# MLP weight sums on VectorE from blocks at hand, and second-product operands split early and kept in DRAM

## The chip, the cores and the metric

The kernel runs on one core of one Trainium2 chip. The metric is the device time of one execution in microseconds (us); smaller is better. The engines are PE (TensorE), DVE (VectorE), ACT (ScalarE), POOL (GpSimd) and SP, which only issues DMAs.

## What is computed

One encoder layer on 512 tokens of width 2048 (16 heads of 128, MLP width 8192), all in float32:

```python
a = rms_norm(x, norm_mix)
h = x + stick_breaking_mixer(a, w_qkv, w_o)
h = h + jnp.square(jax.nn.relu(rms_norm(h, norm_mlp) @ w1)) @ w2
out = rms_norm(h, final_norm)
```

The change touches only the MLP, the third line: a first product of 512x2048 by 2048x8192, a squared ReLU, and a second product of 512x8192 by 8192x2048.

## The kernel before

Every float32 operand of a matmul is split into a high part and a remainder, both rounded to the matmul's type: ACT casts the high part (`whi`, `11h`), DVE subtracts it for the low part (`wlo`, `11l`). A product is then three matmuls, high by high, high by low and low by high (`mm3`, L146 to L150). Attention and its output projection take the first 790 us or so. The MLP follows in two stages.

**Seven products for eight.** Both stages use a Strassen-like scheme: operands are cut in 2x2 blocks, and a unit of work makes seven products of sums of blocks instead of eight of blocks. `ORDER` (L378) lists the seven: the name of the left operand (`11`, `12`, `s1`, `s4`, `s2`, `s3`, `22`), the chain of weights, the PSUM accumulator, and what is added to the weights afterwards. A unit's positions are called p0 to p6 here. Stage 1 (`unit_1`) is 16 units, each 512 of the 8192 columns, 48 matmuls of 256 columns in a product. Stage 2 (`unit_2`) is 8 steps c of two units each (q = 0, 1), 24 matmuls of 512 columns in a product. Units run in order, u0 to u15 and then 16 more; PE runs the products one after the other (`run2`, L437).

**Weights.** A unit loads three of its four weight blocks by SP (`Unit.fetch`): chain a starts with block (0,0) in tile `ra`, b with (1,1) in `rb`, c with (1,0) in `raw`, each as two tiles of 128x1024 (512 KB). `split2` (L409) keeps two products ahead of PE. It casts and subtracts each tile into the pool `wp` of six buffers (a product uses four), and when an entry of `ORDER` says so it adds the next block into the raw tile by an accumulating DMA from POOL's queue:

```python
if more:
    nc.gpsimd.dma_start(raw, u.block(*more, pc), accum_op=ALU.add)
```

So `ra` is p0's weights, and after one, two and three additions those of p2, p4 and p6; `rb` is p3's, and after one addition p5's; `raw` is p1's. A unit has 8 such DMAs. The next unit's tiles are fetched after the splits of p0 (a), p1 (c) and p5 (b).

**Left operands.** In stage 1 they are made once, in 56 of the 72 tiles of the pool `tp`, and stay until u15. A unit's four result blocks go through ReLU and square in `evac_1` (L467) and are stored by ACT's queue to `a_dram` (`store`, L476), 4 tiles of 256 KB. In stage 2 the blocks of step c+1 come back during step c (`mix_a`, L361: tiles `ain`, loaded by SP), and `mix_tasks` (L325) makes the seven operands of each of two halves: four DVE sums (`mix`, L338), seven ACT casts (L332) and seven DVE subtractions (L333). These tasks stand in the list `side`, from which `run2` takes one after each half product. For c = 0 they run during u15, as do the loads of the residual h (`load_h`).

**End.** `load_gain` loads the last norm's gains in the next to last unit, and POOL scales them (L556); `final` (L528) uses POOL too (L535).

The order of each engine's instructions is set at build time by a scheduler which puts them where it expects their inputs to be ready; on the chip each engine and each queue takes its own in order. SP's loads wait there for the buffer they write.

Of the kernel before, what the change touches and what calls it, by code (L numbers as in the profile page):

```python
# [8 lines left out]
F32 = mybir.dt.float32  # L9
F32R = mybir.dt.float32r  # L10
AF = mybir.ActivationFunctionType
ALU = mybir.AluOpType
# [3 lines left out]
P = 128  # L16
S = 512
D = 2048
DF = 8192
# [21 lines left out]
def trunk_kernel(  # L41
# [13 lines left out]
    nc = tc.nc  # L55
# [4 lines left out]
    acc_a = ctx.enter_context(tc.tile_pool(name="acc_a", bufs=4, space=PSUM))  # L60
    dram = ctx.enter_context(tc.tile_pool(name="dram", bufs=1, space=DRAM))
    h_dram = {(tb, n): dram.tile([P, W], F32, name=f"h_{tb}_{n}") for tb in range(NT) for n in range(4)}
    a_dram = {(u, th, kh): dram.tile([P, 2, 256], F32, name=f"a_{u}_{th}_{kh}")
              for u in range(DF // 512) for th in range(2) for kh in range(2)}

    def slot(dt=F32, name="t"):
        return tp.tile([P, W], dt, name=name, tag="t")

    def f(ap):
        return ap.bitcast(F32)  # L70
# [152 lines left out]
    half_in = {}  # L223
    mixed = {}
# [96 lines left out]
    def two(name):  # L321
        return (slot(F32R, name + "h").rearrange("p (i q) -> p i q", q=256),
                slot(F32R, name + "l").rearrange("p (i q) -> p i q", q=256))

    def mix_tasks(key, blocks):  # L325


        got = {}

        def keep(name, a):  # L330
            hi, lo = two(name)
            nc.scalar.copy(hi, a)  # L332
            nc.vector.tensor_tensor(out=lo, in0=a, in1=f(hi), op=ALU.subtract)  # L333
            mixed.setdefault(name, {})[key] = (hi, lo)

        def mix(name, a, b, op):
            t = slot(F32, "mix").rearrange("p (i q) -> p i q", q=256)
            nc.vector.tensor_tensor(out=t, in0=a, in1=b, op=op)  # L338
            got[name] = t

        def s1():
            mix("s1", blocks(1, 0), blocks(1, 1), ALU.subtract)
            keep("s1", got["s1"])

        def s4():
            mix("s2", got["s1"], blocks(0, 0), ALU.subtract)
            mix("s4", blocks(0, 1), got["s2"], ALU.add)
            keep("s4", got["s4"])

        def s3():  # L350
            mix("s3", blocks(0, 0), blocks(1, 0), ALU.subtract)
            keep("s3", got["s3"])

        return [lambda: keep("11", blocks(0, 0)), lambda: keep("12", blocks(0, 1)), s1, s4,
                lambda: keep("s2", got["s2"]), s3, lambda: keep("22", blocks(1, 1))]

    def mix_h(jp):

        return mix_tasks(jp, lambda th, kh: half_in[th, jp + 4 * kh])

    def mix_a(c, pl):  # L361

        got = {}

        def fetch():
            for th, kh in ((0, 0), (0, 1), (1, 0), (1, 1)):
                got[th, kh] = slot(F32, "ain").rearrange("p (i q) -> p i q", q=256)
                nc.sync.dma_start(got[th, kh], a_dram[2 * c + pl, th, kh])

        return fetch, mix_tasks((c, pl), lambda th, kh: got[th, kh])  # L370

# [4 lines left out]
    ORDER = (  # L378
        ("11", "a", "x", (0, 1)),
        ("12", "c", "z", None),  # L380
        ("s1", "a", "y", (1, 1)),
        ("s4", "b", "y", (0, 1)),
        ("s2", "a", "x", (1, 0)),
        ("s3", "b", "x", None),
        ("22", "a", "x", None),
    )
# [20 lines left out]
    done = {"split": 0}  # L407

    def split2(upto):  # L409

        while done["split"] < min(upto, 7 * len(units2)):
            i = done["split"]
            u, (_, chain, _, more) = units2[i // 7], ORDER[i % 7]
            parts = []
            for pc in range(2):
                raw = u.raw[chain, pc]
                hi = wp.tile([P, u.jn, u.width], F32R, name="whi", tag="w")
                lo = wp.tile([P, u.jn, u.width], F32R, name="wlo", tag="w")
                nc.scalar.copy(hi, raw)  # L419
                nc.vector.tensor_tensor(out=lo, in0=raw, in1=f(hi), op=ALU.subtract)  # L420
                parts.append((hi, lo))
                if more:
                    nc.gpsimd.dma_start(raw, u.block(*more, pc), accum_op=ALU.add)  # L423
            ready[i] = parts
            done["split"] += 1
            nxt = units2[i // 7 + 1] if i // 7 + 1 < len(units2) else None
            if nxt:
                if i % 7 == 0:
                    nxt.fetch("a")
                elif i % 7 == 1:  # L430
                    nxt.fetch("c")
                elif i % 7 == 5:
                    nxt.fetch("b")

    side = []
# [30 lines left out]

    def evac_1(u):  # L467

        got = {}

        def tile_of(name):
            if name not in got:
                got[name] = slot(F32, name).rearrange("p (i q) -> p i q", q=256)
            return got[name]

        def store(t, th, kh):  # L476
            nc.scalar.activation(t, t, AF.Square)
            nc.scalar.dma_start(a_dram[u, th, kh], t)

        def go(p, s, ps):  # L480
            if p == 0:
                nc.scalar.copy(tile_of("p1")[:, s, :], ps)
            elif p == 1:
                c = tile_of("p1")
                nc.vector.tensor_tensor(out=c[:, s, :], in0=ps, in1=c[:, s, :], op=ALU.add)
                if s:
                    nc.scalar.activation(c, c, AF.Relu)
                    store(c, 0, 0)
            elif p == 2:
                nc.scalar.copy(tile_of("y1")[:, s, :], ps)  # L490
            elif p == 3:
                got["y", s] = ps
            elif p == 4:
                c = tile_of("u2")
                nc.scalar.copy(c[:, s, :], ps)
                nc.vector.tensor_tensor(out=c[:, s, :], in0=got["y", s], in1=c[:, s, :], op=ALU.subtract)
                if s:
                    nc.scalar.activation(c, c, AF.Relu)
                    store(c, 0, 1)
            elif p == 5:  # L500
                c = tile_of("y1")
                nc.vector.tensor_tensor(out=c[:, s, :], in0=c[:, s, :], in1=ps, op=ALU.subtract)
                if s:
                    nc.scalar.activation(c, c, AF.Relu)
                    store(c, 1, 1)
            elif p == 6:
                c = tile_of("c21")
                nc.scalar.activation(c[:, s, :], ps, AF.Relu)
                if s:
                    store(c, 1, 0)  # L510
        return go
# [34 lines left out]
    def load_h(ns):  # L546
        for n in ns:
            for tb in range(NT):
                hn[tb, n] = slot(F32, "h")
                nc.sync.dma_start(hn[tb, n], h_dram[tb, n])  # L550
# [8 lines left out]
    def first_weights():  # L559
        units2[0].fetch("c")  # L560
        split2(1)
# [25 lines left out]
    for grp in range(4):  # L587
        p = Panel([(w_qkv, 0, 2 * D + grp * W, W)], NK, x_acts, False, evac_v(grp))
        add_panel(p)
        qkv_panels.append(p)  # L590
        for pair in (2 * grp, 2 * grp + 1):
            p = Panel([(w_qkv, 0, pair * 256, 256), (w_qkv, 0, D + pair * 256, 256)], NK, x_acts, True, evac_qk(pair))
# [3 lines left out]
    for n in range(4):  # L596
        p = Panel([(w_o, 0, n * W, W)], NK, o_acts, False, evac_o(n))
# [3 lines left out]
    NC2 = DF // 1024  # L601
# [17 lines left out]
    N1 = DF // 512  # L619
# [151 lines left out]
    with tc.tile_pool(name="acc_b", bufs=4, space=PSUM) as acc_b:  # L771
        pools = {"x": acc_a, "y": acc_b, "z": acc_b}
        run2(0, True, pools, pace=4, only=range(1, 2))
        token_scales()
        run2(0, True, pools, pace=3, only=range(2, 7))
        for u in range(1, N1):
            if u == N1 - 1:
                parts = [mix_a(0, pl) for pl in range(2)]
                for fetch_a, _ in parts:
                    fetch_a()  # L780
                run2(u, True, pools, only=range(2))
                load_h((0, 1))
                side.extend(parts[0][1] + parts[1][1])
                run2(u, True, pools, pace=2, only=range(2, 7))
            else:
                run2(u, True, pools)
        for c in range(NC2):
            for q in range(2):
                if c == 0 and q == 0:
                    side.append(lambda: load_h((2, 3)))  # L790
                if c < NC2 - 1:
                    fetch_a, tasks = mix_a(c + 1, q)
                    side.extend([fetch_a, None, None, None, *tasks])
                elif q == 0:
                    side.append(load_gain)
                run2(N1 + 2 * c + q, False, pools)

# [31 lines left out]
```

## Time and profile before

| | |
|---|---|
| runs | 2105.35, 2106.47, 2109.95 us; median 2106.47 |
| profiled execution | 2111.44 us, span 2109.7 us |
| busy share of the span | PE 98%, DVE 59%, ACT 46%, POOL 17% |
| bytes by DMA | 359.54 MB, of them 134.24 MB on the software queue q0 (POOL's) |

A busy PE is not a PE at its peak: a matmul's record is longer than the step from one matmul to the next, and the granted clock (PEclk, 1.00 is 2.4 GHz, 0.50 is 1.2 GHz) halves the rate without showing as idle time. Both have to be read together. A DMA share of 1.00 means that the 16 DMA engines had a packet under way all the time.

### The profile page before, as it was taken

The numbers are of one execution on the slowest core, as the hardware profiler recorded it, in microseconds if no ns is written. First come the engines' busy times: TensorE is split into PE (matmuls) and PEld (weight loads), VectorE is DVE, ScalarE is ACT, GpSimd is POOL, SyncE is SP. The second block draws the span as 40 slices with busy tenths as digits, with TensorE's granted clock in tenths as the row PEclk, the third lists the DMA queues.
The fourth block names the chain that finished last, engine by engine and source line by source line (L and its number), as shares of the span: only waits on it lengthen the run. The fifth ranks groups of instructions, "written<-read, shape, count | busy, mean of one in ns | idle before, by whom it ended". The sixth has DMA issues, their size and how long they took to land.

```text
span 2109.7 us, 29745 instructions
## 1 busy us (share of the span) xinstructions
PE 2068.1 (98%) x11766; PEld 1816.9 (86%) x11766; DVE 1236.3 (59%) x1501; ACT 973.7 (46%) x1344; POOL 350.0 (17%) x345
## 2 busy tenths in 40 slices
PE   9999999999999998999999999998899999999997
PEld 7888888888888888999999999998678888888786
DVE  7354454453552447444444444447798888888666
ACT  6343343342442346555555555545444444444345
POOL 0000000000000001222222222222222222222433
PEclk9999999999999999999999999999999999999999
DMA  6222222222235347999999999999899999999887
GB/s 197 93 80 80 90 80 80 90 80 90 81 100 190 130 130 154 214 201 218 202 207 206 216 204 205 219 229 258 205 220 225 214 218 229 206 214 228 189 181 160
DMA packets 262172, 359.54 MB, mean 170 GB/s; under 512 B 13696, under 2 KB 161168, under 8 KB 262032
## 3 DMA queue, kind: packets, MB, share of 16 engines
q0 software_dynamic: 102432, 134.24, 40.3%
q1 hardware_dynamic: 144048, 195.07, 27.9%
q10 hardware_dynamic: 15552, 28.32, 3.9%
q8 instruction: 92, 1.51, 0.3%
q14 instruction: 48, 0.39, 0.1%
HBM read 332.41 MB, written 25.17 MB: 169 GB/s over the span
## 4 chain that ended last, share of the span: by engine, by line
PE 77%; DMA 8%; issue 7%; DVE 3%; ACT 2%; POOL 2%; SPq 0%; ACTq 0%; POOLq 0%; DVEq 0%
PE acc L149 25%; PE acc L150 24%; PE acc L148 24%; DMA ra<-w_dram 5%; DMA ain<-a 2%; DVE wlo L420 2%; ACT whi L419 1%; POOL ra L423 1%; PE at L711 1%; POOL rb L423 1%; DMA raw<-w_dram 1%; PE z L149 0%; PE ot L149 0%; PE z L150 0%; PE ot L150 0%
## 5 line engine op out<-in xcount | busy, mean ns | idle before, releaser
L420 DVE TENSOR_TENSOR wlo<-ra,whi 128x1024 fp32r<-128x1024 f32 x256 | 314.6, 1229 | 242.8 <-ACT whi L419 232.7
L419 ACT CAST whi<-ra 128x1024 fp32r<-128x1024 f32 x256 | 268.1, 1051 | 315.3 <-PE acc L149 249.2
L423 POOL DMA_DIRECT2D ra<-w_dram x192 | 241.7, 1259 | 1004.5 <-DVE wlo L420 939.1
L141 DVE TENSOR_TENSOR wlo<-raw,whi 128x1024 fp32r<-128x1024 f32 (+1 forms) x129 | 156.7, 1215 | 265.1 <-ACT whi L140 261.3
L140 ACT CAST whi<-raw 128x1024 fp32r<-128x1024 f32 (+1 forms) x129 | 134.8, 1045 | 262.9 <-PE acc L149 248.0
L420 DVE TENSOR_TENSOR wlo<-rb,whi 128x1024 fp32r<-128x1024 f32 x128 | 157.0, 1227 | 89.6 <-ACT whi L419 87.0
L148 PE MATMUL acc<-thi,whi 128*128 128x512 f32 x512 | 201.0, 393 | 0.0
L150 PE MATMUL acc<-thi,wlo 128*128 128x512 f32 x512 | 199.7, 390 | 0.0
L149 PE MATMUL acc<-tlo,whi 128*128 128x512 f32 x512 | 199.4, 389 | 0.0
L419 ACT CAST whi<-rb 128x1024 fp32r<-128x1024 f32 x128 | 134.4, 1050 | 112.0 <-PE acc L149 84.1
L523 DVE SCALAR_TENSOR_TENSOR h<-acc,stat,h 128x512 f32<-128x512 f32 x224 | 167.0, 746 | 11.1 <-PE acc L150 10.2
L420 DVE TENSOR_TENSOR wlo<-raw,whi 128x1024 fp32r<-128x1024 f32 x64 | 78.3, 1223 | 61.1 <-ACT whi L419 58.0
L150 PEld LDWEIGHTS acc<-thi,wlo 128*128 128x128 f32 x512 | 96.1, 188 | 20.5
L148 PEld LDWEIGHTS acc<-thi,whi 128*128 128x128 f32 x512 | 96.2, 188 | 19.2
L149 PEld LDWEIGHTS acc<-tlo,whi 128*128 128x128 f32 x512 | 96.2, 188 | 19.0
L697 POOL MEMSET rest<- 128x1 f32 x64 | 6.3, 99 | 615.3 <-DVE beta L703 571.4
L148 PE MATMUL acc<-whi,thi 128*128 128x512 f32 x256 | 100.2, 397 | 1.2 <-ACT whi L140 1.2
L148 PE MATMUL acc<-whi,ohi 128*128 128x512 f32 x256 | 101.2, 395 | 0.0
L149 PE MATMUL acc<-wlo,thi 128*128 128x512 f32 x256 | 100.1, 391 | 0.3 <-DVE wlo L141 0.3
L150 PE MATMUL acc<-whi,olo 128*128 128x512 f32 x256 | 100.1, 391 | 0.0
L150 PE MATMUL acc<-whi,tlo 128*128 128x512 f32 x256 | 99.9, 391 | 0.0
L149 PE MATMUL acc<-wlo,ohi 128*128 128x512 f32 x256 | 99.7, 389 | 0.0
(231 smaller groups left out, 5706.6 us busy)
## 6 DMA issues: line engine op xcount, KB each, us to landing
ra<-w_dram POOLq DMA_DIRECT2D x192, 512.0 KB, 7.2
raw<-w_qkv_dram SPq DMA_DIRECT2D x130, 256.0 KB, 2.9
ra<-w_dram SPq DMA_DIRECT2D x64, 512.0 KB, 4.7
rb<-w_dram SPq DMA_DIRECT2D x64, 512.0 KB, 6.4
raw<-w_dram SPq DMA_DIRECT2D x64, 512.0 KB, 5.9
rb<-w_dram POOLq DMA_DIRECT2D x64, 512.0 KB, 7.5
raw<-w_o_dram SPq DMA_DIRECT2D x32, 512.0 KB, 3.8
ain<-a SPq DMA_DIRECT2D x64, 256.0 KB, 6.1
```

Source lines behind the costliest of these rows:

```text
L140: nc.scalar.copy(hi[:, js, :], raw[:, js, :])
L141: nc.vector.tensor_tensor(out=lo[:, js, :], in0=raw[:, js, :], in1=f(hi[:, js, :]), op=ALU.subtract)
L148: nc.tensor.matmul(ps, lhsT=a[0], rhs=b[0], start=start, stop=False, skip_group_check=goes_on)
L149: nc.tensor.matmul(ps, lhsT=a[0], rhs=b[1], start=False, stop=False, skip_group_check=goes_on)
L150: nc.tensor.matmul(ps, lhsT=a[1], rhs=b[0], start=False, stop=stop, skip_group_check=goes_on)
L419: nc.scalar.copy(hi, raw)
L420: nc.vector.tensor_tensor(out=lo, in0=raw, in1=f(hi), op=ALU.subtract)
L423: nc.gpsimd.dma_start(raw, u.block(*more, pc), accum_op=ALU.add)
L523: nc.vector.scalar_tensor_tensor(out=t, in0=ps, scalar=by, in1=t, op0=ALU.mult, op1=ALU.add)
L697: nc.gpsimd.memset(rest[:, 0:1], 0.0)
L711: nc.tensor.transpose(out=ps[:, kb * P : (kb + 1) * P], in_=beta[:, kb * P : (kb + 1) * P], identity=ident)
```

## The change

1. Of the four additions to weights in a unit, two are made by DVE in place of a POOL DMA: chain a takes block (1,1) from `rb` (before `rb` is changed) and block (1,0) from `raw`. `raw` is therefore held until p4's split, and the next unit's is fetched there and no longer after p1's.
2. The seven left operands of stage 2 are made in stage 1, from each unit's four blocks as they come, and stored split: 14 tiles of 256 KB in place of 4, by SP's queue in place of ACT's. Stage 2 loads 28 tiles for each step c in place of 8, and makes no sums, casts or subtractions of left operands.
3. For c = 0 the loads, and those of h, stand between the products of u15, where tiles of stage 1's left operands come free.

```diff
         def s1():
             mix("s1", blocks(1, 0), blocks(1, 1), ALU.subtract)
-            keep("s1", got["s1"])
+            part("s1", got["s1"])
...
+    def mix_a(u, done):
+
+        def keep(name, *parts):
+            for i, t in enumerate(parts):
+                nc.sync.dma_start(a_dram[name, u, i], f(t))
+        return mix_tasks(lambda th, kh: done[th, kh], keep)
+
+    def load_a(c, names):
+        for name in names:
+            for pl in range(2):
+                parts = two(name)
+                for i, t in enumerate(parts):
+                    nc.sync.dma_start(f(t), a_dram[name, 2 * c + pl, i])
+                mixed[name][c, pl] = parts
...
-        ("s1", "a", "y", (1, 1)),
+        ("s1", "a", "y", "b"),
         ("s4", "b", "y", (0, 1)),
-        ("s2", "a", "x", (1, 0)),
+        ("s2", "a", "x", "c"),
...
-                if more:
+                if more in ("b", "c"):
+                    nc.vector.tensor_tensor(out=raw, in0=raw, in1=u.raw[more, pc], op=ALU.add)
+                elif more:
                     nc.gpsimd.dma_start(raw, u.block(*more, pc), accum_op=ALU.add)
...
-                elif i % 7 == 1:
+                elif i % 7 == 4:
                     nxt.fetch("c")
...
             nc.scalar.activation(t, t, AF.Square)
-            nc.scalar.dma_start(a_dram[u, th, kh], t)
+            done[th, kh] = t
+            if (th, kh) == (1, 0):
+                side.extend([tasks[2], None, tasks[3], None, None, tasks[4], None, tasks[5], None])
+            else:
+                side.append(tasks[{(0, 0): 0, (0, 1): 1, (1, 1): 6}[th, kh]])
...
+        steps = [lambda: load_a(0, ("11", "12")), lambda: load_h((0, 1)), lambda: load_a(0, ("s1", "s4")),
+                 lambda: load_a(0, ("s2", "s3")), lambda: load_a(0, ("22",)), lambda: load_h((2,)), lambda: load_h((3,))]
+        for p, load_more in enumerate(steps):
+            run2(N1 - 1, True, pools, only=range(p, p + 1))
+            load_more()
         for c in range(NC2):
             for q in range(2):
...
+                if q and c < NC2 - 1:
+                    for name, *_ in ORDER:
+                        side.extend([lambda name=name, c=c: load_a(c + 1, (name,)), None])
```

How the order of instructions moves, at three places.

**POOL, stage 1.** `ra` and `rb` are the tiles of chains a and b; each row is a run of accumulating DMAs. Before:

```order
L423 DMA ra<-w_dram 128x4x256 x6
L423 DMA rb<-w_dram 128x4x256 x2
L423 DMA ra<-w_dram 128x4x256 x6
L423 DMA rb<-w_dram 128x4x256 x2
L423 DMA ra<-w_dram 128x4x256 x6
```
Now:

```order
L432 DMA rb<-w_dram 128x4x256 x2
L432 DMA ra<-w_dram 128x4x256 x2
L432 DMA rb<-w_dram 128x4x256 x2
L432 DMA ra<-w_dram 128x4x256 x2
L432 DMA rb<-w_dram 128x4x256 x2
```
A unit's six additions to `ra` have become two; those to `rb` stay.

**DVE, from the end of one stage 1 unit into the next.** `wlo` are low parts of weights, L485 and L499 (its new line) evacuate p1, `mix` are sums of left operands, and `y_`, `u_`, `p_`, `c_` result blocks. Before:

```order
L420 TENSOR_TENSOR wlo<-ra,whi 128x1024
L502 TENSOR_TENSOR y_10943<-y_10943,acc_10817 128x256
L420 TENSOR_TENSOR wlo<-ra,whi 128x1024 x2
L420 TENSOR_TENSOR wlo<-raw,whi 128x1024 x2
L420 TENSOR_TENSOR wlo<-ra,whi 128x1024
L485 TENSOR_TENSOR p_11262<-acc_11300,p_11262 128x256
L420 TENSOR_TENSOR wlo<-ra,whi 128x1024
L485 TENSOR_TENSOR p_11262<-acc_11326,p_11262 128x256
L420 TENSOR_TENSOR wlo<-rb,whi 128x1024 x2
```
Now:

```order
L427 TENSOR_TENSOR wlo<-ra,whi 128x1024
L427 TENSOR_TENSOR wlo<-raw,whi 128x1024
L338 TENSOR_TENSOR mix<-c_11338,y_11051 128x512
L333 TENSOR_TENSOR s1l<-mix,s1h 128x512
L338 TENSOR_TENSOR mix<-mix,p_10914 128x512
L338 TENSOR_TENSOR mix<-u_11191,mix 128x512
L427 TENSOR_TENSOR wlo<-raw,whi 128x1024
L333 TENSOR_TENSOR s4l<-mix,s4h 128x512
L427 TENSOR_TENSOR wlo<-ra,whi 128x1024
L430 TENSOR_TENSOR ra<-ra,rb 128x1024
L499 TENSOR_TENSOR p_11407<-acc_11455,p_11407 128x256
```
Between the two halves of p1's weights (`wlo<-raw`, which stood one behind the other) there now stand the sums and the first low part of the left operands, and behind `wlo<-ra` the addition from `rb`.

**SP, from stage 1 into stage 2.** Tiles `a_0_...` are stored blocks, `as_0_...` the stored parts of the operands s1 to s4; 128x4x256 loads are stage 1's weights, 128x2x512 loads stage 2's. Before:

```order
L401 DMA rb<-w_dram 128x4x256 x2
L401 DMA ra<-w_dram 128x2x512 x2
L368 DMA ain<-a_0_0_88 128x512
L368 DMA ain<-a_0_1_89 128x512
L368 DMA ain<-a_1_0_90 128x512
L368 DMA ain<-a_1_1_91 128x512
L368 DMA ain<-a_0_0_92 128x512
L368 DMA ain<-a_0_1_93 128x512
L368 DMA ain<-a_1_0_94 128x512
L368 DMA ain<-a_1_1_95 128x512
L401 DMA raw<-w_dram 128x2x512
L550 DMA h<-h_0_72 128x512
```
Now:

```order
L375 DMA s4h<-as_0_0_184 128x512
L375 DMA s4l<-as_0_1_185 128x512
L375 DMA s4h<-as_1_0_186 128x512
L375 DMA s4l<-as_1_1_187 128x512
L408 DMA raw<-w_dram 128x2x512 x2
L367 DMA as_14_0_276<-s3h 128x512
L367 DMA as_14_1_277<-s3l 128x512
L375 DMA s2h<-as_0_0_216 128x512
L375 DMA s2l<-as_0_1_217 128x512
L375 DMA s2h<-as_1_0_218 128x512
L375 DMA s2l<-as_1_1_219 128x512
L375 DMA s3h<-as_0_0_248 128x512
```
The first `raw` tile of stage 2 stood behind 8 operand loads; now it stands behind 16 operand loads and 8 loads of h (most of them ahead of the rows shown), and more of both follow.

## Rows read from the trace of the kernel before

**Rows 1.** Page, busy time of each engine: us (share of the span) xinstructions.

```profile
PE 2068.1 (98%) x11766; PEld 1816.9 (86%) x11766; DVE 1236.3 (59%) x1501; ACT 973.7 (46%) x1344; POOL 350.0 (17%) x345
```

**Rows 2.** Busy time by stretch; columns PE, PEld, DVE, ACT, POOL, then PEclk, DMA, GB/s.

```profile
790.00:850.00 60.00, 53.67 (x402) 51.87 (x401) 41.54 (x60) 36.70 (x61) 11.50 (x9) 0.94 0.75 159
850.00:1410.00 560.00, 559.93 (x4663) 559.48 (x4662) 266.99 (x278) 300.33 (x402) 142.71 (x111) 1.00 1.02 209
1410.00:1520.00 110.00, 96.88 (x553) 84.95 (x552) 73.85 (x91) 52.83 (x73) 20.98 (x18) 0.92 0.96 241
1520.00:1985.00 465.00, 461.26 (x2023) 378.43 (x2022) 397.86 (x477) 221.25 (x257) 114.68 (x96) 1.00 0.96 219
1985.00:2100.00 115.00, 109.80 (x463) 87.81 (x461) 77.15 (x96) 52.03 (x74) 50.28 (x38) 0.97 0.78 164
```

**Rows 3.** Timeline of PE in stage 2, starts of two products in a row.

```profile
1639.70 0.39 PE L148 MATMUL acc<-whi,s1h 128*128 128x512 f32 x1
...
1645.14 0.39 PE L148 MATMUL acc<-whi,s4h 128*128 128x512 f32 x1
```

**Rows 4.** Waits of PE from 790 to 850: us in total, times, longest.

```profile
PE acc L148 <- ACT hin L318: 3.0, 1, 3.0
PE acc L150 <- DVE wlo L420: 1.9, 3, 1.1
PE acc L148 <- ACT whi L419: 1.4, 1, 1.4
```

**Rows 5.** Chain of work around five stalls: start us, us, what.

```profile
1412.35 14.76 DMA ra<-w_dram
...
1473.20 12.05 DMA ain<-a
...
1621.11 6.16 DMA ain<-a
...
1767.25 9.18 DMA ra<-w_dram
...
1979.65 5.63 DMA gain<-g_fin_dram
...
1992.20 7.87 DMA ra<-w_dram
```

**Rows 6.** Waits of ACT from 1520 to 1985.

```profile
ACT whi L419 <- DMA ra<-w_dram: 18.0, 11, 3.3
...
ACT 11h L332 <- DMA ain<-a: 16.3, 6, 3.3
```

**Rows 7.** DMA queues from 1100 to 1260, then 1540 to 1940: packets, MB, share.

```profile
q0 software_dynamic: 16756, 16.64, 69.7%
q1 hardware_dynamic: 12612, 12.53, 24.4%
...
q0 software_dynamic: 22149, 42.70, 64.1%
q1 hardware_dynamic: 23744, 45.10, 31.6%
```

**Rows 8.** Durations ns min/median/max of one line, then of a tile.

```profile
L639 DVE TENSOR_TENSOR sq<-sq,x x7: 1215/1216/1226, 10.3 to 31.7; 128x1024 f32<-128x1024 f32 x7
...
L368 SPq DMA_DIRECT2D ain<-a x64: 319/418/1428, 1407.4 to 1933.0; - x64
L338 DVE TENSOR_TENSOR mix<-ain x32: 678/684/693, 1434.2 to 1952.9; 128x512 f32<-128x512 f32 x32
L332 ACT CAST 11h<-ain x16: 612/620/622, 1432.4 to 1935.2; 128x512 fp32r<-128x512 f32 x16
```

**Rows 9.** Timeline of ACT at the end of a stage 1 unit.

```profile
1209.39 1.05 ACT L419 CAST whi<-raw 128x1024 fp32r<-128x1024 f32 x1 [0.39 <-PE acc L149]
...
1210.75 0.63 ACT L477 ACTIVATE c<-c 128x512 f32<-128x512 f32 x1
...
1213.71 1.05 ACT L419 CAST whi<-raw 128x1024 fp32r<-128x1024 f32 x1 [0.95 <-PE acc L149]
```

More of the change, by code (lines that the diff above doesn't have):

```diff
@@ L62, in trunk_kernel @@
     h_dram = {(tb, n): dram.tile([P, W], F32, name=f"h_{tb}_{n}") for tb in range(NT) for n in range(4)}
-    a_dram = {(u, th, kh): dram.tile([P, 2, 256], F32, name=f"a_{u}_{th}_{kh}")
-              for u in range(DF // 512) for th in range(2) for kh in range(2)}
+    a_dram = {(name, u, i): dram.tile([P, 2, 256], F32, name=f"a{name}_{u}_{i}")
+              for name in ("11", "12", "s1", "s4", "s2", "s3", "22") for u in range(DF // 512) for i in range(2)}
     def slot(dt=F32, name="t"):
@@ L323, in two, with mix_tasks, part @@
                 slot(F32R, name + "l").rearrange("p (i q) -> p i q", q=256))
-    def mix_tasks(key, blocks):
+    def mix_tasks(blocks, keep):
         got = {}
-        def keep(name, a):
+        def part(name, a):
             hi, lo = two(name)
@@ L333, in keep @@
             nc.vector.tensor_tensor(out=lo, in0=a, in1=f(hi), op=ALU.subtract)
-            mixed.setdefault(name, {})[key] = (hi, lo)
+            keep(name, hi, lo)
         def mix(name, a, b, op):
@@ L347, in s4, with keep @@
             mix("s4", blocks(0, 1), got["s2"], ALU.add)
-            keep("s4", got["s4"])
+            part("s4", got["s4"])
         def s3():
             mix("s3", blocks(0, 0), blocks(1, 0), ALU.subtract)
-            keep("s3", got["s3"])
-        return [lambda: keep("11", blocks(0, 0)), lambda: keep("12", blocks(0, 1)), s1, s4,
-                lambda: keep("s2", got["s2"]), s3, lambda: keep("22", blocks(1, 1))]
+            part("s3", got["s3"])
+        return [lambda: part("11", blocks(0, 0)), lambda: part("12", blocks(0, 1)), s1, s4,
+                lambda: part("s2", got["s2"]), s3, lambda: part("22", blocks(1, 1))]
     def mix_h(jp):
[L359 to L370, printed above, removed]
+        def keep(name, hi, lo):
+            mixed.setdefault(name, {})[jp] = (hi, lo)
+        return mix_tasks(lambda th, kh: half_in[th, jp + 4 * kh], keep)
+    def mix_a(u, done):
[10 more added lines that the diff above has]
+                mixed[name][c, pl] = parts
     ORDER = (
@@ L467, in evac_1 @@
     def evac_1(u):
-        got = {}
+        got, done = {}, {}
+        tasks = mix_a(u, done)
         def tile_of(name):
@@ L776, in trunk_kernel @@
         for u in range(1, N1):
[L777 to L785, printed above, removed]
-                run2(u, True, pools)
+            if u < N1 - 1:
+                run2(u, True, pools)
+        steps = [lambda: load_a(0, ("11", "12")), lambda: load_h((0, 1)), lambda: load_a(0, ("s1", "s4")),
[3 more added lines that the diff above has]
+            load_more()
         for c in range(NC2):
             for q in range(2):
[L789 to L794, printed above, removed]
+                if q and c < NC2 - 1:
+                    for name, *_ in ORDER:
+                        side.extend([lambda name=name, c=c: load_a(c + 1, (name,)), None])
+                elif c == NC2 - 1 and q == 0:
                     side.append(load_gain)
```

## Prediction

> **What bounds the kernel now.** First I read the busy shares: PE is busy 98% of the span, everything else far less [rows 1]. So only time that PE loses can be won, and a whole stage of matmuls cannot shrink, since the change leaves all of them. Then I read the same by stretch [rows 2], and there two losses: idle time (us less PE busy), and the clock (one less PEclk, times us), because a clock granted at 1.2 GHz halves the rate while PE still shows as busy. From 790 to 850, where the MLP starts, that is 6.3 + 3.6 = 9.9 us; in stage 1, 850 to 1410, 0.1 us; where stage 1 hands over to stage 2, 1410 to 1520, 13.1 + 8.8 = 21.9 us; in stage 2 up to 1985 3.7 us; and at the end 5.2 + 3.5 = 8.7 us. All together 44.3 us, 2% of the time, is what there is to win. The clock fell only in stretches in which PE had stood idle for some us; an idle time of 3 us thus costs more than 3.
>
> A product takes 560/4663 x 48 = 5.76 us in stage 1 [rows 2] and 1645.14 - 1639.70 = 5.44 us in stage 2 [rows 3]; a unit of seven is 40.3 and 38.1 us.
>
> Who makes PE wait? At the start it waits 3.0 us for a turned block of h, which the change does not touch, and 1.4 + 1.9 us for weights [rows 4]. In the chain of waits the other stalls end on DMAs [rows 5]: an addition to `ra` that took 14.76 us at 1412; operand loads `ain` of 12.05 us at 1473 and 6.16 us at 1621; an addition of 9.18 us at 1767; at 1979 the load of gains, behind which POOL's next addition was queued and landed only at 1992.20 + 7.87. Inside stage 2 ACT stands still 18.0 us for additions to `ra` and 16.3 us for `ain` [rows 6], and its casts of weights queue behind. The DMA engines are at a share of 1.02 in stage 1 and 0.96 in stage 2 [rows 2].
>
> **Load, before and after.** From the two queues' rows [rows 7], one MB costs the 16 engines 0.244 x 160/12.53 = 3.12 us on SP's queue and 0.697 x 160/16.64 = 6.70 us on POOL's in stage 1; 2.80 and 6.00 us in stage 2. A weight tile is 0.524 MB, an operand tile 0.262. A unit of stage 1 needs now 6 fetches, 4 stores and 8 additions: 4.2 x 3.12 + 4.19 x 6.70 = 41 us of its 40.3, which is the share of 1.02. With 6 fetches, 14 stores and 4 additions it is 6.82 x 3.12 + 2.10 x 6.70 = 35 us, 88%. In stage 2 a unit goes from 36.9 us (97%) to 6.82 x 2.80 + 2.10 x 6.00 = 31.7 us, 83%. More bytes, but less time of the engines.
>
> DVE in stage 1 is busy 267/560 = 48% [rows 2], 19.2 us a unit. It gains 4 additions of 128x1024 (1.22 us, as the like-shaped `sq` sum [rows 8]), 7 subtractions and 4 sums of 128x512 (0.68 us each [rows 8]): 12.4 us, so 31.6 us or 78%. In stage 2 it goes from 86% to 79%: per step of 76.2 us it loses 22 of 0.68 us and gains 8 of 1.22 us. ACT in stage 1 gains 7 casts of 0.62 us [rows 8], 54% to 64%. SP issues 20 DMAs a unit at 0.42 us [rows 8], 8 us: no limit.
>
> **The sum, part by part.**
>
> *Start, 790 to 850: -4 us* of 9.9. The additions for p4 and p6 come from DVE, right behind the split (1.22 us in place of a DMA of 7 to 9 us), so the waits for p4's weights and the second fall of the clock go. What is left is the wait for h and its clock. Bounds: 0 (the waits only come later) and -6.5.
>
> *Stage 1: +1 us* of 0.1. The weak place is p1 of each unit. Its second weight half now stands on DVE behind the new sums. The unit before ends at 1209.3 (the cast at 1209.39 was released by PE [rows 9]) and its last square at 1211.38, 2.1 us later. Then follow on DVE and ACT, each waiting for the other, sum, cast, subtraction and two sums: 4 x 0.68 + 0.62 = 3.4 us, with handovers 5.9 us after the unit's end. The cast that `wlo` needs ends at 5.5 us [rows 9], so `wlo` runs from 5.9 to 7.1 us; PE wants it a quarter into p1, at 5.76 x 1.25 + 0.24 = 7.4 us. A margin of 0.3 us, in each of 15 units. I take 1 us for the lot; bounds 0 and 15 x 0.68 = 10 us (one operation more ahead each time). The other waits have a product's time or more: p2's addition is still a DMA, but with DMAs at 88% it should not land later than now, and now it costs nothing.
>
> *Handover, 1410 to 1520: -7 us* of 21.9. From the end of u15's p0 to the end of stage 2's first unit are 72.7 us. In that time SP must move 28 + 16 loads, 19 stores and 8 weight tiles, 20.7 MB, 58 to 65 us of the engines; 6 additions are 3.15 MB, 19 us. That is 77 to 84 us, over by 4 to 11. Counted in the same way the kernel before had 32 loads, 4 stores, 8 weight tiles (13.6 MB) and 14 additions (7.3 MB): 38 + 44 = 82 us. So the jam is about as large as it was, and weights stand in it behind 24 loads. What improves is who suffers: two additions in a unit can come late in place of four, and ACT no longer waits for operands. I take 15 us left. Bounds: 0 left (-22), or twice today's loss (+22), if the 14.76 us of [rows 5] become the rule for weights too.
>
> *Stage 2: -3 us* of 3.7. Both causes of [rows 6] go; p2's and p5's additions stay. Bounds 0 and -3.7.
>
> *End: -4.7 us* of 8.7. Gains still hold up POOL, but what stands behind them is now the addition for p5, a product later than p4's, and a shorter jam. Bounds 0 and -7.
>
> The sum is -4 + 1 - 7 - 3 - 4.7 = -17.7. The profiled execution took 2111.4 us and would be 2093.7; it lies 5.0 us above the median of the runs, 2106.5, so the prediction is **2089 us**.
>
> One rule speaks against the end's term. Rows first: POOL's issue of an addition takes 142.71/111 = 1.29 us where DVE is 48% busy and 114.68/96 = 1.19 us where it is 86% [rows 2], so a fuller DVE does not slow it. The Trainium skill, "SBUF — State Buffer", section "Who interferes with whom", says that a DVE operation with two SBUF inputs holds off a GpSimd operation that reads SBUF; issuing does not count, in agreement with these rows, but the four scalings of gains do, and by that rule each could wait for one addition of 1.22 us, 4.9 us that would eat the end's gain: 2094 in place of 2089. I keep 2089, as DVE as a whole gets emptier there.
>
> **Rivals.**
>
> *A. The jam decides: slower, 2118.5 us, chance 0.11.* At the handover each weight fetch stands in SP's queue behind 2 MB or more of operands, and all of step 1's 28 loads follow before the next unit's. If the loss there is twice today's, about 45 us, the other terms (-10.7) are outweighed by +23. It decides from 33 us lost on. For it: the chain of 1412 and 1473. Against: the total is no larger than before.
>
> *B. DVE is late in stage 1: no change, 2106 us, chance 0.10.* If each of 15 units loses one 1.2 us operation at p1, that is 18 us, the whole gain. For it: a margin of 0.3 us. Against: today DVE is 86% busy in stage 2 and the losses there end on DMAs.
>
> *C. The handover runs clean: 2076 us, chance 0.20.* If additions under way cost the engines no more than other bytes, the 23.9 MB need 23.9 x 2.80 = 67 us of 72.7, and the term is -20 in place of -7. For it: the cost per MB of an addition may be waiting, not work. The Trainium skill, "DMA: Bandwidth & Descriptors", section "Specifications", gives a core some 358 GB/s of HBM; by bytes alone 23.9 MB would be 67 us, the same. Against: shares near 1 at only 209 to 241 GB/s [rows 2].
>
> *D. The additions that stay are the late ones: 2101.5 us, chance 0.11.* p2's is the one at 1412. If start and handover give nothing and stage 2 half, 1 - 1.5 - 4.7 = -5.
>
> That the change doesn't do what it says is ruled out: POOL's rows show four additions a unit for eight.
>
> **How the numbers follow.** The forecast has 0.48. A measurement can tell about 0.2% from no change, 4.2 us. Faster: forecast, C and 0.09 of D, 0.77; same: B and the rest of D, 0.12; slower: A, 0.11. The range goes from 2069 (C with its bounds) to 2107 (D, B); A and a little below C are left out.
>
> **What would show it.** Right: by the same reckoning, some 6 us lost up to 850, under 3 us in stage 1, some 15 around the handover, under 2 in stage 2, 4 at the end; DMA shares near 0.9 and 0.85; DVE at 78% and 79%; no wait of ACT for a left operand. Wrong: PE waiting for `wlo<-raw` in each unit of stage 1 (B), or a clock of 1.2 GHz for more than 25 us after 1410 with `raw`, `ra` or `rb` loads of over 12 us (A).

## The result and the profile after

The kernel with the change took 2122.51 us (median of 5 runs, 2115.33 to 2123.36), the kernel before, run beside it, 2108.58 (5 runs, 2105.35 to 2109.95). The ratio is 1.006, 95% interval 1.004 to 1.008: slower by 0.6%, where 2089 had been predicted. The profiled execution took 2123.21 us, 11.8 more than the profiled one before.

The page after the change, busy time of each engine, to be held against [rows 1]:

```profile
PE 2071.3 (98%) x11766; PEld 1814.9 (86%) x11766; DVE 1389.6 (66%) x1629; ACT 971.5 (46%) x1344; POOL 194.1 (9%) x217
```

POOL's time fell from 350 to 194 us and DVE's grew by 153, as meant. The same stretches as in [rows 2], columns PE, PEld, DVE, ACT, POOL, then PEclk, DMA, GB/s (the DMA share adds up the times of packets over 16 engines, so it can come out above 1.00):

```profile
790.00:850.00 60.00, 51.60 (x375) 49.96 (x374) 45.77 (x66) 36.63 (x63) 4.56 (x5) 0.91 0.49 123
850.00:1410.00 560.00, 558.11 (x4638) 556.65 (x4637) 425.36 (x485) 345.58 (x496) 70.43 (x55) 1.00 0.85 220
1410.00:1520.00 110.00, 100.99 (x617) 88.57 (x616) 78.91 (x89) 53.16 (x68) 12.35 (x10) 1.00 1.05 330
1520.00:1985.00 465.00, 449.27 (x1928) 364.17 (x1929) 355.95 (x371) 167.49 (x161) 54.94 (x46) 0.99 0.82 231
1985.00:2110.00 125.00, 122.48 (x534) 99.61 (x533) 102.62 (x120) 57.09 (x77) 40.46 (x28) 1.00 0.54 129
```

The DMA shares came out as forecast (0.85 and 0.82), and still PE lost more in stage 2: 15.7 us idle where it was 3.7. By the prediction's reckoning (idle time, plus the clock) the change loses 3.3 us more than before over all five stretches, not 11.8. The reckoning is blind to a part: a matmul's record lasts 0.39 us and the next one starts 0.23 us later, so a stall can show as 0.16 us shorter than it is, and many are short. The starts of the units miss nothing. In PE's timeline of the change a unit of stage 2 begins with its first matmul on `11h`:

```profile
1588.56 0.39 PE L148 MATMUL acc<-whi,11h 128*128 128x512 f32 x1
...
1629.04 0.39 PE L148 MATMUL acc<-whi,11h 128*128 128x512 f32 x1
...
1670.96 0.39 PE L148 MATMUL acc<-whi,11h 128*128 128x512 f32 x1
```

These two units took 40.5 and 41.9 us, so against seven undisturbed products (38.1 us) they lost 2.4 and 3.8. Adding this up over all units, with 40.3 us for one of stage 1 and the last unit up to the last matmul, gives this table (us lost; the kernels E1 to E9 are the experiments below, in the order in which they ran, each in its profiled execution). "Handover" is u15 and the first two units of stage 2. In E3 the first matmuls of some units run ahead of the end of the unit before; there a unit counts from where it goes on, and by its first matmul 6 us would move from the handover to the next 11 units. E1 and E5, and E6 and E9, have nearly the same order of instructions in those 11 units and still differ there by 1.8 and 2.9 us, so less than 3 us in that column tells nothing by itself.

```
                      u0   u1-u14  handover  next 11 units  last 3   all
before               12.5    0.7     23.0         5.9          9.8   51.9
the change           16.2    3.8     15.4        25.0          4.2   64.6
E1 spread loads      16.0    2.4     14.6         5.9          6.3   45.2
E2 no loads          16.1    3.1     11.8         0.0          4.2   35.2
E3 sums only         13.8    0.0     17.5         6.3          8.7   46.3
E4 operands only     12.0   29.3     33.4        57.0          9.3  141.0
E5 first unit        11.2    4.4     14.7         7.7          4.9   42.9
E6 all three         12.2    0.7     12.4         4.5          5.8   35.6
E7 half the loads    16.2    2.0     16.0         1.0          4.2   39.4
E8 add later         16.2    0.0     10.2        10.9          4.2   41.5
E9 spread, later     16.2    0.0     10.4         1.6          6.7   34.9
```

The change loses 12.7 us more than before; with an MLP that starts 1.1 us earlier (792.0 for 793.1) that is the difference of the two profiled executions to 0.2 us. All of it and more is in the 11 middle units of stage 2. There PE waits for weights, in the waits of PE from 1520 to 1985, and ACT waits for both tiles that POOL adds to, in the waits of ACT there (us in total, times, longest):

```profile
PE acc L149 <- DVE wlo L427: 9.6, 13, 0.8
PE acc L148 <- ACT whi L426: 4.3, 8, 1.0
```

```profile
ACT whi L426 <- DMA rb<-w_dram: 30.7, 12, 4.0
ACT whi L426 <- DMA ra<-w_dram: 27.9, 10, 3.8
```

All 22 of these waits end on an addition from POOL, none on a fetch by SP, which has the same name in this view. Before, ACT waited 18.0 us for `ra` there [rows 6], with three times as many additions to it, and for `rb`, with as many additions as now, hardly at all:

```profile
ACT whi L419 <- DMA rb<-w_dram: 4.0, 6, 2.2
```

**Where the loads stand.** The 28 operand loads of a step are not spread over its two units. In SP's instructions of the line `load_a`, by tile (count, ns min/median/max, first and last start; two neighbouring stretches), those of one step begin with the first row and end with the second:

```profile
L375 SPq DMA_DIRECT2D 11h<-a x2: 319/328/338, 1592.6 to 1594.0; - x2
...
L375 SPq DMA_DIRECT2D 22l<-a x2: 320/564/807, 1628.5 to 1631.7; - x2
```

All lie between 1592.6 and 1631.7, nearly all in the unit that began at 1588.56, the second of its step, in which the tiles of the step's own operands come free. By unit the DMA engines and the landing of POOL's additions alternate. Windows of the change by unit (columns as above), loading unit, other unit, and so on:

```profile
1588.60:1629.00 40.40, 38.85 (x169) 31.34 (x168) 30.69 (x33) 14.58 (x14) 4.77 (x4) 1.00 0.89 256
1629.00:1671.00 42.00, 40.33 (x170) 32.65 (x170) 30.92 (x33) 14.70 (x15) 4.77 (x4) 0.96 0.68 180
1671.00:1710.10 39.10, 38.41 (x170) 31.46 (x169) 30.76 (x33) 14.67 (x15) 4.77 (x4) 1.00 0.92 267
1710.10:1749.30 39.20, 38.44 (x170) 31.46 (x169) 30.85 (x33) 14.66 (x15) 4.79 (x4) 1.00 0.71 189
```

The accumulating DMAs (line 432) of the change, first from 1588.6 to 1631, then from 1637 to 1675, from issue to landing:

```profile
DMA to landing us min/median/max: 6.2/10.2/10.9
```

```profile
DMA to landing us min/median/max: 6.1/6.1/6.2
```

Beside the loads an addition takes 10.2 us (median), without them 6.1. The late ones end on the chain of waits of the change (1600 to 1650), in which a 10.8 us addition holds the cast, and the cast the low part:

```profile
1606.34 10.79 DMA rb<-w_dram
1617.23 1.06 ACT whi L426
1618.31 1.24 DVE wlo L427
```

What lands late is wanted in either unit. The two additions for p2 of the unit that begins at 1629.04 were issued at 1626.62 and 1630.25, behind the loads, and landed after 10.2 and 10.9 us; ACT waited 6.1 us for them, and p2 took 9.3 us (1639.92 to 1649.20) in place of 5.4. That is why the unit without loads lost more (3.8 us) than the one with them (2.4).

### The profile page after: what moved, and what is told of

It reads as the page before. It is cut to its first block, busy times and chain, and to the rows that moved or that the text cites. A ratio compares the mean times of both kernels' runs of the same rounds, so it can differ in the third digit from the quotient of the medians.

```text
span 2121.2 us, 30309 instructions
## 1 busy us (share of the span) xinstructions
PE 2071.3 (98%) x11766; PEld 1814.9 (86%) x11766; DVE 1389.6 (66%) x1629; ACT 971.5 (46%) x1344; POOL 194.1 (9%) x217
## 4 chain that ended last, share of the span: by engine, by line
PE 46%; issue 40%; POOL 5%; DMA 5%; DVE 2%; ACT 1%; POOLq 0%; SPq 0%; ACTq 0%
PE acc L149 14%; PE acc L150 14%; PE acc L148 14%; DMA rb<-w_dram 3%; POOL rb L432 3%; POOL ra L432 3%; DVE wlo L427 1%; DMA ra<-w_dram 1%; PE at L725 1%; ACT whi L426 1%; DMA s3h<-as 1%; PE z L149 0%; PE ot L149 0%; PE z L150 0%; PE ot L150 0%
## 5 line engine op out<-in xcount | busy, mean ns | idle before, releaser
L432 POOL DMA_DIRECT2D ra<-w_dram x64 | 79.4, 1240 | 791.9 <-DVE wlo L427 693.1
L432 POOL DMA_DIRECT2D rb<-w_dram x64 | 79.5, 1249 | 457.2 <-DVE wlo L427 410.8
L426 ACT CAST whi<-raw 128x1024 fp32r<-128x1024 f32 x64 | 67.4, 1052 | 64.1 <-PE acc L149 62.2
```

## The experiments

Three theories were open at first. Bunching: the loads stand in one of two units, and the additions beside them land late. DVE: the additions on DVE delay the low parts of weights, whatever the loads do. Volume: there are more bytes in all, and it does not matter where they stand.

**E1, loads spread.** A step's loads stand in both of its units, 14 in each. The scheduler sets SP's order, so to hold them there each waits for a one-column copy on DVE behind the last residual update.

```diff
-                if q and c < NC2 - 1:
-                    for name, *_ in ORDER:
-                        side.extend([lambda name=name, c=c: load_a(c + 1, (name,)), None])
+                if c < NC2 - 1:
+                    todo = [(name, pl) for name, *_ in ORDER for pl in range(2)]
+                    for name, pl in todo[7 * q : 7 * q + 7]:
+                        side.extend([lambda name=name, pl=pl, c=c: load_a(c + 1, (name,), (pl,))] + [None] * (c > 0))
...
+                    if c:
+                        nc.vector.tensor_copy(t[:, 0, 0:1], latest[-1][:, 0:1])
                     nc.sync.dma_start(f(t), a_dram[name, 2 * c + pl, i])
```

> The changed kernel, with the 28 operand loads of each step spread over both units of the step before: each load is tied to a residual update by a one-column DVE copy into its tile, so it cannot start earlier. Bunching theory (all 28 loads fall into one of two units, the accumulating DMAs of weights in flight there take 9.5 to 11 us in place of 6, and PE waits for p2's and p5's weights): with 31.7 us of DMA work in each unit of 38.1 the additions land in 7 to 8.5 us everywhere, the loss from 1520 on falls from some 20 us to under 8, and the time from 2122 to about 2108, no slower than before. DVE theory (the additions on DVE delay the low parts of weights, loads do not matter): no better than 2122, a few us worse for the 28 extra copies a step. Volume theory (more bytes in all, however spread): all additions at 8.5 us or more, about 2116.

Measured: 2102.60 us, ratio to before 0.9975 (0.9964 to 0.9986), some 20 us less than the change (18.8 when each is taken against the kernel before that ran beside it), and 5 less than the bunching theory expected. Two units of E1 in windows:

```profile
1585.10:1623.70 38.60, 38.47 (x170) 31.52 (x170) 32.35 (x47) 14.74 (x15) 4.77 (x4) 1.00 0.83 231
1623.70:1662.50 38.80, 38.53 (x169) 31.33 (x168) 32.17 (x47) 14.47 (x14) 4.77 (x4) 1.00 0.83 231
```

The share is now 0.83 in both, the average that the prediction had reckoned with, and the 11 middle units lose 5.9 us in place of 25.0. But for 28 one-column copies a step on DVE, the work, the bytes and the mean share are the same: what differs is their place in time. From 1540 to 1985 an addition lands after 6.1 us at least, 8.2 in the median and 10.4 at most, where it was 6.0, 7.8 and 11.4 in the change: the spreading does not make the additions faster in the middle, it takes away the latest ones. From 1520 to 1985 ACT still waits 51.4 us for them, little less than the 58.6 of the change, so most of such a wait costs PE nothing. What costs is presumably the part beyond the lead of the two products that are split ahead; that was not measured by itself. The volume theory, which had 2116 us, and the DVE theory as it stood (2122 or more) fail.

**E2, no loads, and E7, half of them.** E2 uses step 0's operands in every step. E7 loads 14 of the 28 in their old places.

```diff
             for pl in range(2):
+                if c:
+                    mixed[name][c, pl] = mixed[name][0, pl]
+                    continue
```

For E7 the condition is `if c and pl:`.

> The changed kernel, with the operand loads of stage 2 left out after the first step (steps 1 to 7 use the operands of step 0, so this part of the computation is left out). Bunching and volume theories: additions land in 6 to 6.5 us, the waits for p2's and p5's weights after 1560 go, about 2104. DVE theory: the waits stay, about 2120.

> The changed kernel, with 14 in place of 28 operand loads in each step after the first, bunched as in the change (one of the two halves uses the operands of step 0, so this part of the computation is left out). Bunching theory: the second unit of a step has 31.7 us of DMA work in 38.1 as in the spread kernel, the additions there land in 7.5 to 9 us, and the time is between that of no loads (2096) and the change (2122), near 2104. If the number of bytes sets the loss in proportion, 2109.

E2 and E7 leave the other steps' operands out of the computation. Measured: E2 2096.02 us, ratio 0.9947 (0.9932 to 0.9962); E7 2098.89 us, ratio 0.9955 (0.9942 to 0.9968). Both came out below what had been expected of the bunching theory (2104 each). E2's stage 2 in the windows has no idle time at all:

```profile
1520.00:1985.00 465.00, 465.00 (x2053) 385.06 (x2052) 376.36 (x392) 179.57 (x171) 60.23 (x50) 1.00 0.59 137
```

Half the loads give back 23.6 of the 26.5 us that all give back. The loss is not in proportion to the bytes (that would have been 2109): with 14 loads beside them the additions still come nearly in time, and the 11 middle units lose 1.0 us.

**E3 and E4, one part of the change alone.** E3 is the kernel before with DVE's two additions; E4 is the change with all four additions by DMA. The fetch of `raw` goes with the additions, after p4's split in E3 and after p1's in E4.

```diff
 E3, on the kernel before
-        ("s1", "a", "y", (1, 1)),
+        ("s1", "a", "y", "b"),
-        ("s2", "a", "x", (1, 0)),
+        ("s2", "a", "x", "c"),
...
 E4, on the change
-        ("s1", "a", "y", "b"),
+        ("s1", "a", "y", (1, 1)),
-        ("s2", "a", "x", "c"),
+        ("s2", "a", "x", (1, 0)),
```

> The kernel before, with only the first part of the change: two of the four additions to weights by DVE; left operands as before. Bunching theory: no additions over 8.5 us in stage 2 after 1520, as 8 operand loads a step do not bunch; DVE is then at some 98% in stage 2, so the low parts may be late there, 2095 to 2112. DVE theory: the worst kernel of all, over 2130, since DVE has all its old work and the additions too. Start of the MLP: if the additions on DVE cost the start, its loss of some 14 us shows here too.

> The changed kernel with the first part undone: all four additions by POOL's DMA, left operands split early and kept in DRAM. Bunching theory: a unit with 28 loads has 29.4 + 25.1 = 54 us of DMA work in 38.1, so some 16 us lost in each of seven steps, 2200 or more; its additions take 12 us and longer. DVE theory: DVE is relieved, 2105 or less.

Measured: E3 2106.00 us, ratio 0.9989 (0.9980 to 0.9999), by itself hardly to be told from no change; E4 2200.16 us, ratio 1.0438 (1.0423 to 1.0454). The DVE theory had over 2130 for E3 and 2105 or less for E4, the bunching theory 2200 or more for E4. E3's stage 2, then E4's stage 1 and stage 2 in windows:

```profile
1520.00:1985.00 465.00, 460.09 (x2015) 376.00 (x2014) 442.34 (x518) 222.17 (x253) 57.18 (x48) 1.00 0.65 163
```

```profile
850.00:1410.00 560.00, 542.74 (x4444) 535.07 (x4442) 344.10 (x411) 331.28 (x475) 134.94 (x105) 1.00 1.11 261
...
1520.00:1985.00 465.00, 425.22 (x1767) 334.03 (x1767) 278.04 (x296) 153.85 (x148) 99.18 (x83) 0.98 1.04 272
```

The part with the operands costs 93 us (2200.16 against 2107.45 of the kernel before beside it) where the DMA engines have no room (shares of 1.11 and 1.04); the part with the sums makes that room (E3: 0.65 in place of 0.96 in stage 2), at the price of DVE at 95% there. Alone, the second part is a loss and the first about nothing.

**E5, first unit by POOL.** E1, with u0's two additions as DMAs again.

```diff
+            if i < 7:
+                more = {"b": (1, 1), "c": (1, 0)}.get(more, more)
```

> The spread kernel (2102.6 us), with the first unit's four additions all by POOL's DMA again. If the additions on DVE cost the start of the MLP (DVE is full there with the sums of h, and the loss from 790 to 850 was 13.9 us in place of 9.9), that loss goes back to about 10 us and the time to 2098.5. If the start is lost to the sums of h alone, it stays at 14 us and 2102.6.

Measured: 2102.94 us, ratio 0.9978 (0.9966 to 0.9990), no different from E1. u0 does lose 4.8 us less than in E1, but 3.8 are lost again in u1 to u14 and in the 11 middle units. Whether the start's loss counts could not be told here.

**E6, one addition later.** What made the first `rb` addition late? On DVE the change puts the second half of `ra<-ra,rb` ahead of the first half of `rb`'s low part; the DMA that adds to `rb` waits for that low part. DVE and POOL in the timeline of the change:

```profile
1600.94 1.22 DVE L430 TENSOR_TENSOR ra<-ra,rb 128x1024 f32<-128x1024 f32 x1
1602.08 1.22 DVE L427 TENSOR_TENSOR wlo<-rb,whi 128x1024 fp32r<-128x1024 f32 x1
```

```profile
1603.60 1.19 POOL L432 DMA_DIRECT2D rb<-w_dram  x1 [12.62 <-DVE wlo L427]
```

E6 is E5 with these two the other way round (the second half of `rb` has its own DMA, which comes after both):

```diff
-                    nc.vector.tensor_tensor(out=raw, in0=raw, in1=u.raw[more, pc], op=ALU.add)
+                    def add(raw=raw, other=u.raw[more, pc]):
+                        nc.vector.tensor_tensor(out=raw, in0=raw, in1=other, op=ALU.add)
+                    if more == "b" and pc:
+                        waiting.append(add)
+                    else:
+                        add()
                 elif more:
                     nc.gpsimd.dma_start(raw, u.block(*more, pc), accum_op=ALU.add)
+                if chain == "b" and waiting:
+                    waiting.pop()()
```

> The same as the run with the first unit's additions on POOL, and in all other units the second half of the addition from rb stands behind the first half of the split of rb on DVE, so that the first addition to rb by DMA starts some 1.2 us earlier. If p5's weights are late because of the order on DVE, the waits at p5 in stages 1 and 2 (some 9 us in the spread kernel) fall by half or more, about 2093. If they are late only because DMAs are slow, 2098.5 as the run beside it.

Measured: 2093.89 us (2089.33 to 2095.94), ratio 0.9931 (0.9919 to 0.9943), faster than both kernels.

**E8, the later addition alone, and E9, with the loads spread but u0 as in the change.** E8 is the change with E6's last edit and nothing else; E9 is E6 without E5's lines.

> The change with one thing more: the second half of the addition from `rb` to `ra` stands on DVE behind the first half of rb's low part, so that the first accumulating DMA to `rb` need not wait for it. The loads stay bunched in each step's second unit. If the two causes are independent, what the later addition gave on top of the spread loads (2102.94 to 2093.89, 9 us) comes off the change's 2122.5 as well: about 2113.5, and stage 2 still loses some 11 us of the 20. If late additions come from the bunched loads alone, the later addition is worth 0 to 3 us here: 2119 to 2122. If the time on DVE is the whole cause and the bunching matters only because the addition starts late, it comes near the spread version with it, 2094 to 2100.

> Loads spread over both units and the later addition, the first unit's additions on DVE as in the change. Against the version that has all three (2093.89), this prices the first unit's part, which alone could not be told from nothing (2102.6 to 2102.94). If what the start loses on DVE is passed on, 4 to 5 us of the start come back: about 2098. If it is lost again anyway, 2094.

Measured: E8 2102.07 us (2100.22 to 2105.27), ratio 0.9975 (0.9966 to 0.9985); E9 2098.01 us (2093.89 to 2100.40), ratio 0.9955 (0.9939 to 0.9971). None of the three cases written down for E8 holds. The later addition is worth 20 us alone and spread loads are worth 20 us alone, but the two together give 24.5, so they are no independent sums. Both act on the same losses, as the products that start between 1540 and 1960 show (us over 5.44 each, added up by position; the other positions lose nothing in these kernels):

```
                      p2    p4    p5
the change          12.8   2.8   8.2
E1 spread loads      0.8   0.2   5.0
E8 add later         8.1   0.0   2.9
E6 all three         3.7   0.0   0.8
E9 spread, later     1.5   0.0   0.1
```

The spreading takes most at p2, the order on DVE most at p5, and each takes a part at the other place. The timeline of E8 at the place shown for E6, then POOL's issue:

```profile
1593.89 1.22 DVE L429 TENSOR_TENSOR wlo<-rb,whi 128x1024 fp32r<-128x1024 f32 x1
1595.02 1.22 DVE L433 TENSOR_TENSOR ra<-ra,rb 128x1024 f32<-128x1024 f32 x1
```

```profile
1595.40 1.19 POOL L439 DMA_DIRECT2D rb<-w_dram  x1 [11.48 <-DVE wlo L429]
```

From the cast of `rb`'s first half (at 1599.42 in the change, 1592.36 in E8) to this issue it is 4.2 us in the change and 3.0 in E8. The second addition to `rb` is issued 6.9 us after that cast in both. So the two stand 3.9 us apart, not 2.7, and land after 7.3 and 9.8 us, not 9.6 and 10.8. ACT's waits for the two tiles in stage 2 show what each edit reaches, in E8, then E1, then E9, then E6:

```profile
ACT whi L428 <- DMA ra<-w_dram: 27.7, 11, 3.0
ACT whi L428 <- DMA rb<-w_dram: 19.5, 7, 4.9
```

```profile
ACT whi L428 <- DMA rb<-w_dram: 36.7, 17, 2.9
ACT whi L428 <- DMA ra<-w_dram: 14.7, 8, 2.5
```

```profile
ACT whi L430 <- DMA ra<-w_dram: 14.4, 8, 2.5
...
ACT whi L430 <- DMA rb<-w_dram: 4.9, 2, 3.3
```

```profile
ACT whi L432 <- DMA ra<-w_dram: 23.9, 11, 3.7
ACT whi L432 <- DMA rb<-w_dram: 16.2, 5, 3.9
```

Beside the change's 30.7 (`rb`) and 27.9 (`ra`), the order on DVE lowers the wait for `rb`, the spreading that for `ra`. With both, E9 waits little for `rb`, E6, with the same order of instructions there, 16.2 us: these sums scatter between executions, and what PE lost by position says more. E8 also removes what u1 to u14 lost (3.8 us to 0.0) and a third of the handover's loss. Stage 1 before u15 has no operand loads, and there all kernels with the change's order on DVE lost 2.0 to 4.4 us (E1, E2, E5, E7), those with E6's 0.0 to 0.7, so there the order was a cause without any operand loads. But it takes full DMA engines too: E3, with the same order on DVE at a share of 0.69 in place of 0.85, lost nothing there.

E9 and E6 differ in u0's additions alone: 4.1 us by the medians, but nothing in the profiled executions, whose spans are 2092.9 and 2093.5 (u0 loses 4.0 us less in E6, the rest 4.7 more). With intervals that overlap, what the start is worth stays open.

## Why the prediction was wrong

By its own terms, with what the units' starts measured:

| term | predicted | measured |
|---|---|---|
| start | -4 | +3.7 |
| stage 1 | +1 | +3.1 |
| handover | -7 | -7.6 |
| stage 2 | -3 | +19.1 |
| end | -4.7 | -5.6 |

**Stage 2 is the step that failed: "-3 us of 3.7", with "bounds 0 and -3.7".** It came from the load: "in stage 2 a unit goes from 36.9 us (97%) to ... 31.7 us, 83%". The mean is right (0.82 measured), but it is a mean over a step of two units. The 28 loads all stand in the second: 10.5 MB of weights and operands and 2.1 MB of additions by the same prices are 10.5 x 2.80 + 2.10 x 6.00 = 42 us of 38.1, the other unit 21. (Measured by the windows above it was 0.89 x 40.4 = 36 us and 0.68 x 42.0 = 29, as a part of the loads moves only in the next unit.) The diff said so (`if q and c < NC2 - 1`), and a reckoning by unit would have put the forecast's sign in doubt. "p2's and p5's additions stay" was the right place to look; that they cost nothing was never tested against the loads beside them. A bound of 0 on the side of the loss excluded a loss without a reason. By the prediction's own reckoning, idle time and clock, this term came out at +16.7. With the loads spread (E1) it is 0.0, still not -3: the 5.9 us that are left in E1 fall to 1.6 in E9 and 4.5 in E6, with the order on DVE.

The second half of the cause was read and not followed. The rows of the order showed `ra<-ra,rb` on DVE, but only its price of 1.22 us was counted. That it stands ahead of a low part for which a DMA waits, and so delays a product three places later, was not.

**Start.** "The additions for p4 and p6 come from DVE ..., so the waits ... go" was wrong in sign, and outside its bounds of 0 and -6.5. PE's waits there went up, from [rows 4] to this, 790 to 850 of the change:

```profile
PE acc L148 <- ACT hin L318: 3.0, 1, 3.0
PE acc L150 <- DVE wlo L427: 2.9, 3, 1.4
PE acc L148 <- ACT whi L426: 2.4, 2, 1.4
```

In u0 DVE also makes stage 1's left operands, and the four additions stand in that row of work. E5 takes them out of it, and u0 loses 4.8 us less than in E1; E3, with the additions but without the new operands of stage 2 beside them, loses 13.8 us there, between the 12.5 before and the change's 16.2. So the additions are a cause of what u0 loses; what that is worth for the whole is not shown.

**Stage 1.** The size was small, as said, but the place was not p1 (rival B's). In the change 3.6 us of the loss lie at p5 and nothing at p1, and with E8's order it went to zero.

**Handover and end** were right in size: 15.4 us left where "I take 15 us left" stood, at a share of 1.05. At the handover that is in part luck. By the prediction's own reckoning 9.0 us were left there and not 15, and 5.2 of the 15.4 go with the order on DVE (10.2 in E8), which its sum did not have. At the end the reason given fits what happened: the unit in which the gains are loaded and scaled, the third from the end, lost 6.8 us before and nothing in the change. Rival C's clean handover did not come. Rival A had a total near the truth (2118.5) for a wrong reason, as the handover lost less than before. Rival D named the mechanism, "the additions that stay are the late ones", but priced it as a smaller gain.

**The rule on the gains' scalings** would have added 4.9 us at the end. The four scalings before, in the change and in E1, where they run a unit later (ns min/median/max, first and last start):

```profile
L556 POOL TENSOR_SCALAR gain<-gain x4: 1509/3024/3185, 1985.5 to 1990.8; 128x512 f32<-128x512 f32 x4
```

```profile
L570 POOL TENSOR_SCALAR gain<-gain x4: 1577/2028/2390, 2001.1 to 2007.4; 128x512 f32<-128x512 f32 x4
```

```profile
L575 POOL TENSOR_SCALAR gain<-gain x4: 1487/1500/1635, 2011.5 to 2019.7; 128x512 f32<-128x512 f32 x4
```

Spans on POOL are rough. In E1 a scaling takes 1.5 us, and three of the four beside DVE's additions and subtractions in the change take 1.8 to 2.4: 2.0 us more in all, under half of the 4.9. In the same stretch one subtraction on DVE took 1.63 us in place of 1.22 (1.61 beside a scaling of E1), so either side came out longer. That agrees in kind with what the Trainium skill, "SBUF — State Buffer", section "Who interferes with whom", lets one expect, at a smaller price; the rule was not tried by itself. Before, beside the subtractions of that kernel, the scalings took up to 3.2 us, so the change did not make them longer. The reason for which the prediction set the rule aside, that DVE "gets emptier there", was wrong: in the last stretch DVE is busy 102.62 us of 125 (82%), where it was 77.15 of 115 (67%) [rows 2].

## What to carry to other kernels

Work out the load of the DMA engines for the shortest stretch in which the transfers must land, by where the queue will put them, not as a mean over a period: spreading the same loads was worth 20 us of 2122 here. Then look for work on one engine that stands ahead of what a DMA waits for: moving one 1.22 us addition behind a subtraction gave as much. Two such causes may share one slack, so the repairs must be tried together and apart (20, 20, and 24.5 us), and the losses are best measured by the starts of units, since idle time and clock together showed only 3.3 of 11.8 us.

## What the runs showed that was not expected

- An accumulating DMA of 512 KB landed after 6.1 us without the operand loads and after 10.2 us (median) beside them, at a DMA share of only 0.89 over that unit.
- The handover moved 330 GB/s for 110 us, at a share of 1.05, and lost less than before at 241 GB/s and 0.96 [rows 2].
- The part that alone cost 93 us (E4) and the part that alone gave about nothing (E3) make together, with the order and the spreading mended and u0's two additions back on POOL, the fastest version (E6, 2093.89 us, 0.7% under before).
